# One queue in program order: TensorE's matmuls issued as the program emits them

## The chip, the cores and the metric

The kernel runs on one core of a Trainium2 chip. The metric is the device time of one execution in microseconds (us): the median of three runs, and beside it one profiled execution with its trace. A core has engines that run side by side, each with a queue of its own that it works through from front to back: TensorE (PE in the profile; its weight loads are listed as PEld), VectorE (DVE), ScalarE (ACT), GpSimd (POOL) and SyncE (SP, which here issues the DMAs). An instruction that has to wait for another engine holds up everything behind it in its own queue.

## The reference

Two layers of a hybrid backbone over 256 latent and 256 context tokens of width 1024, all in float32. The core of one layer is this:

```python
def _layer(xl, xc, mod_l, mod_c, P, rope_a, rope_b, ctx_out):
    ...
    hl = _rmsnorm(xl, P['norm_mix']) * (1 + sc1) + sh1
    hc = _rmsnorm(xc, P['norm_mix']) * (1 + csc1) + csh1
    y_l, y_c = _mixer(hl, hc, P, rope_a, rope_b, ctx_out)
    xl = xl + g1 * y_l
    xl = xl + g2 * _conv_ffn(_rmsnorm(xl, P['norm_ffn']) * (1 + sc2) + sh2, P)
    ...
```

`_mixer` makes one input projection, feeds it to three token mixers (A: windowed attention with a sink, 8 heads; B: latent attention, 8 heads; C: gated linear attention in both directions), projects each mixer's output, merges the three by sigmoid gates and projects once more. `_conv_ffn` is an up-projection to 5632 columns, a width-3 convolution over the tokens, silu times value, and a down-projection. In the second (last) layer only the latent tokens are finished, so its later stages run on 256 columns where those of the first run on 512.

## The kernel before

**Work.** Activations lie with features on the 128 partitions and tokens along the columns. Almost all of TensorE's work is `mm3` (lines 171 to 174): a float32 product is made of three products of high and low parts, `whi` by `hh`, `whi` by `hl` and `wlo` by `hh`, so lines 172, 173 and 174 hold three matmuls each time. `load_w` (158) fetches a weight tile by DMA into a ring, ACT casts it to its high part (`whi`, 164) and DVE or POOL subtracts for the low part (`wlo`, 168). `unit` (176) is one output tile: 4 or 8 blocks of 128 rows, three matmuls each, into one bank of PSUM. An activation is split in the same way (`split`, 187).

**Stages of a layer, in the program's order.** The modulation and norm with the first seven output tiles of the input projection (380 to 397); the gated linear attention (434 to 755), with its gates at 537 to 549, where for each of two `t` and two directions `d` a matmul (541) writes half of a PSUM pair that ACT (543) and DVE (544) read; attention A and attention B (796 to 914, called at 983 and 987); the third merge (992); the output projection (1025 to 1039); the up-projection with convolution (`inner`, 1116) and the down-projection (1141 to 1152). A norm is spread over its neighbours as steps: `sums` (228, matmuls of line 233), a chain of small DVE operations (`rsqrt`, 192, and line 239), `spread` (241, the matmul of line 242), then `hmod` for each of 8 tiles.

**What sets the order.** The program emits its instructions in the order of its Python loops. A scheduler then fixes each engine's queue: it goes through the instructions with a machine model, prefers the one emitted first, and lets a later one go ahead on an engine while the earlier one's inputs are not ready by that model. So a queue of the kernel before is the program's order, except where a later instruction overtook. `tc.issue_after(ins)` pins some DMAs and DVE operations of the modulation behind one named instruction; it doesn't name TensorE's.

**Attention's order.** `scores` (803) emits the matmuls of lines 813 and 817 and the softmax behind them on DVE and ACT (819 to 834). `values` (837) emits the transposes of the probabilities (850), which ACT and DVE turn into `pth` (854) and `ptl` (855); `outputs` (858) emits their products (866, 869). `fills` are units of the gates and branch products (`merge`, 771), laid between them by hand:

```python
for i, stp in enumerate(steps + [None]):
    if stp is not None:
        scores(*stp)
        ...
        step_on()
        ...
    pv = values(*steps[i - 1]) if i else None
    for n in range(nfill[i]):
        fills.pop(0)()
        if n == 0 and pv:
            pv()
            pv = None
        ...
```

`pv` is `outputs` of the step before; `step_on` emits the next head's keys, values or queries. So the program's order is: scores of this step, transposes of the step before, one fill, outputs, one more fill.

The change touches the function below and, by the queue that it sets, every matmul that `hybrid` emits.

## Time and profile before

| what | value |
|---|---|
| median of 3 runs | 1519.2 us (1518.48 to 1521.23) |
| profiled execution | 1519.25 us |
| its span, first to last instruction | 1517.5 us |
| TensorE (PE) busy | 1438.5 us, 95% |
| VectorE (DVE) busy | 1218.2 us, 80% |
| ScalarE (ACT) busy | 811.7 us, 53% |
| GpSimd (POOL) busy | 494.6 us, 33% |
| DMA | 213 MB, 139 GB/s over the span |
| mean granted clock of TensorE | 0.981 |

The profiled execution lies 0.05 us from the median, and 1.75 us of it lie outside the span. Busy time counts an engine's own instructions. A timeline lists one engine's instructions in the order of time, so it shows the queue itself; where an engine sat idle before an instruction, the row says for how long and what released it. "PEclk" is the granted share of TensorE's 2.4 GHz: 1.00 or 0.50 in a stretch.

### The profile page before, as it was taken

Reading aid. Unit: us, or ns where it says so; the run is one execution under the profiler, and the core shown is the slowest. Engines: PE = TensorE matmul, PEld = TensorE weight load, DVE = VectorE, ACT = ScalarE, POOL = GpSimd, SP = SyncE. Lnnn points to the kernel's source line nnn. Section 1 sums busy time; section 2 is a strip of 40 time slices with the busy share of each in tenths; the row PEclk is TensorE's granted clock in tenths of the full one; section 3 lists DMA queues with packets and bytes.
Section 4 is the critical chain, followed back from the end, with each engine's and each line's share of the span. In section 5 each row is a group of like instructions: output and inputs, shape, how many; then the busy total and the mean of one; then the engine's idle time right before and its main releaser. Section 6 shows DMA issues by size and latency. Waiting matters only on the chain. (4 is left out here: it accounts for less than half of the span.)

```text
span 1517.5 us, 27758 instructions
## 1 busy us (share of the span) xinstructions
PE 1438.5 (95%) x10062; PEld 1243.2 (82%) x10062; DVE 1218.2 (80%) x2289; ACT 811.7 (53%) x1698; POOL 494.6 (33%) x407
## 2 busy tenths in 40 slices
PE   6988999999999899999999999988989899989997
PEld 4766867778788799788888889967878889989997
DVE  5688597786888979798877979978777886897886
ACT  4565355565653346534244235675466776665663
POOL 0065233233320001446544640034354443133231
PEclk9999999999999999999999999999999999999999
DMA  8411122222236575444645865532132235556553
GB/s 315 169 50 62 46 76 78 72 74 77 84 105 224 178 229 182 139 158 149 214 139 157 289 232 153 182 105 79 56 102 85 89 108 186 179 163 198 175 172 93
DMA packets 107432, 213.28 MB, mean 141 GB/s; under 512 B 12000, under 2 KB 21600, under 8 KB 106272
## 3 DMA queue, kind: packets, MB, share of 16 engines
q1 hardware_dynamic: 106608, 210.86, 42.6%
q8 instruction: 79, 1.29, 0.3%
q10 hardware_dynamic: 688, 0.66, 0.1%
q14 instruction: 57, 0.47, 0.1%
HBM read 210.42 MB, written 1.05 MB: 139 GB/s over the span
## 5 line engine op out<-in xcount | busy, mean ns | idle before, releaser
L168 POOL TENSOR_TENSOR wlo<-raw,whi 128x512 fp32r<-128x512 f32 (+1 forms) x270 | 373.8, 1390 | 711.5 <-ACT whi L164 464.0
L164 ACT CAST whi<-raw 128x512 fp32r<-128x512 f32 (+1 forms) x614 | 360.5, 597 | 320.0 <-PE ps_mm L173 136.4
L172 PE MATMUL ps_mm<-hh,whi 128*128 128x512 f32 (+1 forms) x808 | 298.3, 369 | 11.7 <-ACT cvr L473 8.5
L173 PE MATMUL ps_mm<-hl,whi 128*128 128x512 f32 (+1 forms) x808 | 292.7, 362 | 0.0
L174 PE MATMUL ps_mm<-hh,wlo 128*128 128x512 f32 (+1 forms) x808 | 292.4, 362 | 0.2 <-DVE wlo L168 0.2
L168 DVE TENSOR_TENSOR wlo<-raw,whi 128x512 fp32r<-128x512 f32 (+1 forms) x344 | 238.1, 703 | 44.0 <-ACT whi L164 39.3
L172 PEld LDWEIGHTS ps_mm<-hh,whi 128*128 128x128 f32 x808 | 155.4, 192 | 38.9 <-ACT cvr L473 8.7
L174 PEld LDWEIGHTS ps_mm<-hh,wlo 128*128 128x128 f32 x808 | 154.9, 192 | 26.0 <-DVE wlo L168 0.6
L173 PEld LDWEIGHTS ps_mm<-hl,whi 128*128 128x128 f32 x808 | 155.4, 192 | 23.8 <-issue 0.4
L104 DVE SCALAR_TENSOR_TENSOR jk<-wm,sil 128x1024 f32<-128x1024 f32 x112 | 172.8, 1543 | 1.5 <-DMA wm<-wmod 0.4
L172 PE MATMUL ps_pair<-hh,whi 128*128 128x512 f32 (+1 forms) x312 | 109.8, 353 | 2.0 <-DVE cy L1092 1.7
L174 PE MATMUL ps_pair<-hh,wlo 128*128 128x512 f32 (+1 forms) x312 | 109.0, 352 | 0.3 <-DVE wlo L168 0.2
L173 PE MATMUL ps_pair<-hl,whi 128*128 128x512 f32 (+1 forms) x312 | 109.2, 351 | 0.0
L854 ACT CAST pth<-ps_pair 128x512 fp32r<-128x512 f32 (+1 forms) x96 | 49.4, 515 | 38.7 <-PE ps_pair L850 26.9
L172 PEld LDWEIGHTS ps_pair<-hh,whi 128*128 128x128 f32 x312 | 58.5, 188 | 11.6 <-ACT whi L164 3.2
L174 PEld LDWEIGHTS ps_pair<-hh,wlo 128*128 128x128 f32 x312 | 58.4, 188 | 9.6 <-DVE wlo L168 0.7
L855 DVE TENSOR_TENSOR ptl<-ps_pair,pth 128x512 fp32r<-128x512 f32 (+1 forms) x96 | 57.4, 597 | 10.8 <-ACT pth L854 10.2
L173 PEld LDWEIGHTS ps_pair<-hl,whi 128*128 128x128 f32 x312 | 58.6, 188 | 8.7
L172 PE MATMUL ps_mm<-ach,whi 128*128 128x256 f32 (+1 forms) x200 | 63.7, 319 | 1.2 <-ACT ach L1125 0.7
L173 PE MATMUL ps_mm<-acl,whi 128*128 128x256 f32 (+1 forms) x200 | 63.5, 317 | 0.0
L174 PE MATMUL ps_mm<-ach,wlo 128*128 128x256 f32 (+1 forms) x200 | 63.4, 317 | 0.0
L174 PE MATMUL ps_mm<-mh,wlo 128*128 128x256 f32 x192 | 55.4, 289 | 4.7 <-DVE wlo L168 4.7
(673 smaller groups left out, 3582.2 us busy)
## 6 DMA issues: line engine op xcount, KB each, us to landing
raw<-wup SPq DMA_DIRECT2D x184, 256.0 KB, 3.0
raw<-win SPq DMA_DIRECT2D x182, 256.0 KB, 2.7
wm<-wmod SPq DMA_DIRECT2D x72, 512.0 KB, 3.9
raw<-wdn SPq DMA_DIRECT2D x88, 256.0 KB, 2.9
raw<-wbr SPq DMA_DIRECT2D x48, 256.0 KB, 2.6
raw<-wout SPq DMA_DIRECT2D x48, 256.0 KB, 3.0
wm<-wm SPq DMA_DIRECT2D x8, 1024.0 KB, 8.1
x<-xT SPq DMA_DIRECT2D x16, 256.0 KB, 4.8
```

The costliest lines, as they stand in the source:

```text
L104: V.scalar_tensor_tensor(out=jk, in0=wm, scalar=1.0, in1=sil[:, s], op0=ALU.mult, op1=ALU.mult, accum_out=MOD[l][:, s, t:t + 1])
L164: S.copy(hi[:, :ncols], raw[:, :ncols])
L168: e.tensor_tensor(out=lo[:, :ncols], in0=raw[:, :ncols], in1=hi[:, :ncols].bitcast(F32), op=ALU.subtract)
L172: mm(o, ah, bh, start=start, stop=False)
L173: mm(o, ah, bl, start=False, stop=False)
L174: mm(o, al, bh, start=False, stop=stop)
L854: S.copy(dh, tv)
L855: V.tensor_tensor(out=dl, in0=tv, in1=dh.bitcast(F32), op=ALU.subtract)
```

## The change

TensorE's whole queue is issued in the order in which the program emits its matmuls. The other engines' queues, and the DMAs', are still made by the scheduler, now against that order. No instruction is added or taken away in the source.

```diff
--- before.py
+++ after.py
@@ -1286,7 +1286,7 @@
     arrays = _pack(inputs)
     aps = {k: nc.dram_tensor(k, a.shape, mybir.dt.from_np(a.dtype), kind="ExternalInput").ap() for k, a in arrays.items()}
     out = nc.dram_tensor("out", (KT, 128, T), F32, kind="ExternalOutput").ap()
-    with tile.TileContext(nc) as tc:
+    with tile.TileContext(nc) as tc, tc.manual_schedule(engines={mybir.EngineType.PE}):
         hybrid(nc, tc, aps, out)
     r = run_bass_kernel_spmd(nc, [arrays], core_ids=[0])
     o = r.results[0]["out"]
```

## Rows read from the trace of the kernel before

**Rows 1.** TensorE's waits: line, releaser: us in total, times, longest

```profile
PE ps_o L242 <- DVE dg L239: 8.1, 5, 3.6
PE ps_pair L850 <- DVE ptl L855: 1.7, 2, 1.5
PE ps_pair L172 <- DVE cy L1092: 1.7, 1, 1.7
```

**Rows 2.** Busy us by stretch: length, PE, PEld, DVE, ACT, POOL, PEclk, DMA share, GB/s

```profile
215.00:470.00 255.00, 250.25 (x1315) 203.98 (x1314) 195.04 (x416) 151.70 (x364) 75.93 (x63) 1.00 0.29 93
1085.00:1236.00 151.00, 134.74 (x978) 120.78 (x977) 125.03 (x242) 100.97 (x241) 65.37 (x49) 0.98 0.28 91
```

**Rows 3.** Timeline (start us, us, engine, line, operation) of PE, attention A of layer 0

```profile
222.20 0.50 PE L172 MATMUL ps_mm<-hh,whi 128*128 128x512 f32 x1
...
223.55 1.06 PE L850 MATMUL ps_pair<-cst,p 128*128 128x128 f32 x8 [0.15 <-DVE ptl L855]
```

**Rows 4.** Timeline of PE, the last such place of attention B, layer 0

```profile
447.82 0.28 PE L813 MATMUL ps_pair<-kh,q 96*128 96x256 f32 x1
...
448.31 0.45 PE L869 MATMUL ps_o<-ptl,vb 128*64 128x256 f32 x2
```

**Rows 5.** Timeline of PE, the spread of two norms

```profile
590.13 0.28 PE L172 MATMUL ps_pair<-hh,whi 128*128 128x256 f32 x1
...
592.61 0.67 PE L242 MATMUL ps_o<-dg,ones 128*128 128x256 f32 x2
...
968.90 0.70 PE L242 MATMUL ps_o<-dg,ones 128*128 128x256 f32 x2 [0.24 <-DVE dg L239]
```

**Rows 6.** Timeline of PE, the start of the last down-projection of layer 0

```profile
921.85 0.28 PE L172 MATMUL ps_pair<-ach,whi 128*128 128x256 f32 x1
...
925.94 0.39 PE L172 MATMUL ps_mm<-ach,whi 128*128 128x256 f32 x1 [0.69 <-ACT ach L1125]
```

**Rows 7.** Timeline of PE, the way into attention A of layer 1

```profile
1084.37 0.47 PE L172 MATMUL ps_mm<-hh,whi 128*128 128x256 f32 x1
...
1089.18 0.44 PE L749 MATMUL ps_pair<-cst,osb 128*128 128x128 f32 x2 [1.94 <-DVE osb L717]
...
1095.71 0.86 PE L813 MATMUL ps_pair<-kh,q 128*128 128x512 f32 x2
...
1102.91 0.73 PE L813 MATMUL ps_pair<-kh,q 128*128 128x512 f32 x2 [2.19 <-ACT p L828]
```

**Rows 8.** Timeline of PE and DVE where attention A hands over to B, layer 1

```profile
1166.60 0.39 PE L172 MATMUL ps_mm<-ych,whi 128*128 128x256 f32 x1 [0.37 <-ACT m L778]
...
1170.92 1.04 PE L850 MATMUL ps_pair<-cst,p 128*128 128x128 f32 x8
...
1169.27 0.74 DVE L782 SCALAR_TENSOR_TENSOR m<-m,ps_mm 128x256 f32<-128x256 f32 x2
1170.01 0.69 DVE L855 TENSOR_TENSOR ptl<-ps_pair,pth 128x512 fp32r<-128x512 f32 x1
```

**Rows 9.** Timeline of PE, DVE and ACT, the gates of layer 0

```profile
71.83 0.63 PE L541 MATMUL ps_pair<-cg,wg 96*128 96x512 f32 x2
...
74.40 0.47 PE L541 MATMUL ps_pair<-cg,wg 96*128 96x512 f32 x1
...
73.57 1.41 DVE L544 TENSOR_SCALAR mn<-ps_pair,pp 128x512 f32<-128x512 f32 x2 [0.38 <-ACT lab L543]
...
76.59 2.01 ACT L546 ACTIVATE lab<-lab 128x1024 f32<-128x1024 f32 x2
...
84.35 0.79 PE L172 MATMUL ps_mm<-hh,whi 128*128 128x512 f32 x1 [4.05 <-ACT cvr L473]
```

**Rows 10.** Busy us by stretch at the lower clock: first, last, sum of ten

```profile
83.30:90.10 6.80, 5.75 (x14) 4.49 (x15) 6.80 (x7) 2.87 (x7) 5.85 (x4) 0.50 0.00 0
...
1339.40:1342.80 3.40, 3.40 (x18) 3.40 (x18) 2.72 (x8) 2.11 (x6) 0.00 (x0) 0.50 0.02 6
sum 51.00, PE 45.65 PEld 37.42 DVE 44.46 ACT 21.20 POOL 22.35; mean PE 4.56 PEld 3.74 DVE 4.45 ACT 2.12 POOL 2.24
```

## The prediction

> **What bounds the kernel now.** I read the page's list of engines first: TensorE is busy 1438.5 of 1517.5 us, DVE 1218.2, nothing else above 53%. So TensorE has 79 us of idle time in the whole span, and only what changes its queue's idle time or its clock can change the time by much. Then TensorE's waits: they are many and short, and come from DVE and ACT chains, such as the norm's `dg` or the `ptl` that frees a pair of banks [rows 1]. Then the stretches: the attention of layer 0 has TensorE busy 250.25 of 255 us, that of layer 1 only 134.74 of 151, with DVE at 125.03 [rows 2]. Last the whole timeline of TensorE, laid beside the loops: where does the queue leave the program's order? In 48 stretches that hold 1,111 of its 9,059 matmuls; the other 7,948 stand where the program emits them, and the change moves none of them against its neighbours. In nearly every one of the 48 the pattern is that of [rows 3]: by the program the transposes (850) of the step before come next, and the fill unit (172 to 174) after them; in the queue the fill's first matmuls went ahead at 222.20, and the transposes followed at 223.55, as soon as DVE's `ptl` (855) had freed their pair. The fill covered the wait.
>
> **The change part by part.** Nothing is added or removed. Each overtaking matmul goes back behind the one it overtook. Its price is: the moment at which the overtaken matmul's inputs were ready in the trace, less the moment at which TensorE would reach it. The overtakers then run after it instead of during its wait, so on a busy TensorE the wait is lost. It comes back only if TensorE later waits for something that hasn't moved. The queues of DVE, ACT, POOL and SP hold the same instructions; that their order stays is my assumption, bounded below.
>
> Layer 0's attention, nine places. First [rows 3]: reached at 222.1, ready at about 223.5, so 1.4 lost (1.6 with the rest of that place). Last [rows 4]: the second output's `ptl` products are reached at 447.82, where scores went ahead, and start at 448.31: 0.5. All nine worked like this: 1.6, 3.0, 2.9, 0.9, 0.8, 1.5, 2.5, 0.6, 0.4, together 14.2. TensorE is 98% busy here [rows 2], so little can give it back: the wait of 1.7 for `ptl` outside these places [rows 1] and 0.4 of another. I take 12.1.
>
> Norms, two. `spread` of the first is reached at 590.13, and runs at 592.61 when `dg` is ready [rows 5]: 2.4 lost. Its `sums` wait 1.1 us too, but that wait is inside the 2.4, since `dg` follows from `sums`, which start when they did. The second ends at 968.90 in the same way: 2.7, and 0.8 for low parts of weights that come late around it. After the first norm TensorE waits for `cy` 1.7 us and 0.5 for a low part, and DVE's chain towards them starts no later than before [rows 1]; I give back 2.0. Sum 3.9.
>
> The last down-projection of layer 0. By the program its first tile is finished before the second begins; its last block needs `ach`, the last of `inner`. In the queue the second and third tile ran from 921.85, and the block followed at 925.94 [rows 6]. Now TensorE waits the 4.1 us and then has those 27 matmuls still to do: 3.6 after what it waited anyway.
>
> Layer 1's attention. From 1084.37 gate units ran ahead of the transposes of line 749, ready at 1089.18; scores of the first step are ready at 1095.7, those of the second at 1102.91, after 2.2 us of idle time already [rows 7]. These moments hang on DVE and ACT, not on the fills, so the waits don't add up: counted from the second scores, what is left to run puts TensorE 3.6 us behind at 1106.5, not the 9.1 of the two places each by itself. Nine more places follow; the largest is [rows 8], where a product and scores went ahead of transposes ready at 1170.75 and reached at 1166.1: 4.7, less 0.7 that TensorE waited there already. The nine sum to 9.9. But here TensorE is idle 16.3 of 151 us, with DVE at 83% [rows 2], so most of a delay meets a wait that it shortens: I keep a third, 3.3. Sum 6.9, with 13.5 as the upper end.
>
> The gates. For each `t` two matmuls (541) write the halves of a pair; the second half's wait for DVE's reading of the first (544) [rows 9]. Before, both first halves ran at 71.83 and the second halves at 74.40 and 75.18. In program order the second `t` starts only after the first's second half, so ACT and DVE make two rounds one after the other: exp (546) moves from 76.59 to about 77.8, and with it the copy that TensorE waits 4.05 us for [rows 9]. The two stalls of 2.3 us are swallowed by that wait; its end moves by 1.2. Twice, for two layers: 2.4.
>
> The rest (first stage 0.7, both linear attentions 1.8 and 0.5, up-projection of layer 1 0.5, where a delay of 1.4 meets an idle stretch before 1339): 3.5. Four places cost nothing, since the overtaken matmul was ready when reached.
>
> The clock. In ten stretches the granted clock was 0.50, that is 1.2 GHz, each behind a longer or repeated idle time; TensorE was busy 45.65 us of them [rows 10], so half, 22.8 us, is what the low clock cost. New waits of 4.1 [rows 6] and 4.7 [rows 8] are as long as the 4.05 [rows 9] ahead of the first of these stretches. I add two stretches like the one at 1339 (3.40 busy, 1.7 lost [rows 10]): 3.4; the bounds are 0 and five such, 8.5. The Trainium skill's page "TensorE: Matmul & The Clock Gate" (What's actually happening) says that for modelling, the cost of ramping up the clock is under 1% of a typical span. The trace doesn't agree: 22.8 us are 1.5% here. By the page this term would be left out and the forecast would be 3.4 us lower.
>
> Sum: 12.1 + 3.9 + 3.6 + 6.9 + 2.4 + 3.5 + 3.4 = 35.8. One deduction: with fills later, their evacuations no longer stand ahead of the awaited step in DVE's queue, as `m` (782, 0.74 for two) does just ahead of `ptl` in [rows 8]. I take 0.7 off at each of the six waits above 2.5 us: 4.2. That leaves 31.6, on the profiled execution's 1519.25 (0.05 from the median): 1551.
>
> **The rivals.** *Given back*: DVE's chains set the pace, and TensorE's delays in one place shorten its waits in the next. For it: layer 1's 16.3 idle us, and DVE at 80% overall. Against it: TensorE is 98% busy in layer 0's attention, where the largest term lies. If half of the 14.2 and all of layer 1's but 2 us come back, and no clock is lost: 7 + 2 + 2 (norms) + 1.5 + 2.4 + 2 = 17 at most, near 5 at least; about 1530. *Compounding*: each place costs what it does alone, so all 50.7 us of the 48 places are kept, and five stretches of low clock come on top, 8.5: about 1578. *Faster*: the awaited chains get shorter by more than TensorE waits. Scores and transposes reach ACT and DVE ahead of the fills' casts and evacuations, in layer 1's attention above all. It decides where a ready moment comes earlier by more than the wait costs, 1 us at a typical place; if it removes all new waits and half of layer 1's 16.3 idle us, the time is 1519 less 8, 1511. Against it: the awaited moments of [rows 7] follow from matmuls that no fill overtook. *No change*: the order held back nothing that matters, or what is lost is just regained; 1519.
>
> **How the numbers follow.** Forecast (1537 to 1564): 0.56. Given back (1523 to 1537): 0.19. Compounding (above 1564): 0.12. Faster: 0.07. No change within 0.2% (3 us, about what a measurement of this kernel can tell from none): 0.06. So slower 0.87, same 0.06, faster 0.07. For 8 in 10 I leave out faster, no change and the upper half of compounding, 0.19: 1523 to 1577.
>
> **What would show it.** The matmul count stays, and the rows of line 850 come right behind those of 813 and 817 in each step. TensorE's idle time rises from 79 to about 110 us, with most of the rise at lines 850, 869, 242, 172 behind `ach` 1125, and 541 behind 544; stretches at the low clock rise from ten to twelve. The wait for `cvr` (473) gets shorter, and the exps of line 546 later by about 1.2 us. The forecast is wrong if layer 0's attention (from its first scores to the first matmul of line 992's merge) is no longer than before, if DVE's and ACT's queues come out in another order where TensorE waits, or if layer 1's attention grows by more than 14 us.

## The result, and the profile after

The changed kernel takes 1577.5 us (1576.1 to 1579.3) against 1518.8 us before: a ratio of 1.0385, interval 1.0367 to 1.0403, so 58.6 us slower. The forecast was 1551 with 1523 to 1577: right in sign and on where the waits come from, 26 us too low, and just outside the range.

The page of the changed kernel:

```profile
span 1574.6 us, 27756 instructions
PE 1457.9 (93%) x10062; PEld 1259.4 (80%) x10062; DVE 1208.5 (77%) x2289; ACT 815.9 (52%) x1698; POOL 489.0 (31%) x407
```

The span grew by 57.1 us. TensorE's idle time is 116.7 us (1574.6 less 1457.9) where it was 79.0: 37.7 of the 57.1. The other 19.4 us are *busy* time, with the same 10,062 matmuls. Something made the matmuls themselves slower. Two views tell where, and by what.

First, busy time by stage. Columns as in [rows 2]. The stretches end at the same instruction in both traces: gates to first turn (749), the way from there to the first transposes (850), attention of layer 0, then gates to first turn of layer 1, and way in and attention of layer 1. The kernel before:

```profile
71.80:196.10 124.30, 113.75 (x1464) 91.20 (x1462) 95.86 (x170) 64.61 (x123) 55.20 (x56) 0.93 0.18 58
196.10:216.90 20.80, 18.65 (x81) 14.11 (x82) 18.89 (x26) 10.93 (x22) 9.53 (x8) 0.92 0.21 67
216.90:455.50 238.60, 233.85 (x1238) 190.86 (x1237) 184.71 (x400) 144.08 (x351) 74.03 (x62) 1.00 0.26 82
...
993.00:1089.20 96.20, 85.70 (x926) 70.01 (x925) 72.47 (x167) 52.99 (x119) 38.66 (x57) 0.93 0.21 70
1089.20:1246.50 157.30, 142.98 (x1047) 129.12 (x1048) 129.08 (x246) 107.68 (x256) 68.93 (x50) 0.98 0.29 93
```

The changed kernel, the same stages:

```profile
72.90:202.20 129.30, 114.37 (x1463) 91.67 (x1461) 95.29 (x170) 64.91 (x122) 54.81 (x55) 0.93 0.18 54
202.20:230.20 28.00, 21.05 (x81) 15.62 (x81) 18.12 (x28) 11.76 (x23) 10.10 (x8) 0.82 0.21 65
230.20:487.70 257.50, 243.83 (x1238) 198.69 (x1237) 180.52 (x398) 144.71 (x351) 72.97 (x62) 0.95 0.25 75
...
1033.10:1132.70 99.60, 83.67 (x908) 68.40 (x906) 69.46 (x163) 52.56 (x117) 36.55 (x56) 0.93 0.21 65
1132.70:1302.60 169.90, 147.87 (x1064) 133.16 (x1065) 128.87 (x248) 108.71 (x257) 69.75 (x51) 0.95 0.29 86
```

Length less PE gives the idle time of a stage. It rose by 4.4, 4.8, 8.9, 5.4 and 7.7 us in these five. In the attention of layer 0 the same 1,238 matmuls are busy 10.0 us longer, and the granted clock there is 0.95 instead of 1.00. In layer 1's the busy time rose by 4.9, but 17 matmuls more fall into that stage now, and the stage ahead of it has 18 fewer and is 2.0 us less busy. That leads to the second view, the stretches at 0.50 (1.2 GHz), five of seventeen and their sum, against [rows 10]:

```profile
211.80:218.60 6.80, 5.07 (x12) 3.37 (x13) 5.62 (x10) 1.62 (x4) 0.00 (x0) 0.50 0.11 39
269.80:276.60 6.80, 5.96 (x18) 5.07 (x19) 5.74 (x15) 2.17 (x7) 0.00 (x0) 0.50 0.15 40
423.40:440.40 17.00, 14.26 (x50) 11.88 (x49) 10.65 (x21) 8.64 (x19) 1.28 (x1) 0.50 0.12 30
...
955.90:962.70 6.80, 4.82 (x21) 4.52 (x22) 3.37 (x7) 2.07 (x4) 0.00 (x0) 0.50 0.36 109
...
1218.70:1222.10 3.40, 2.82 (x14) 2.85 (x15) 1.26 (x3) 0.59 (x1) 0.42 (x1) 0.50 0.74 220
...
sum 102.00, PE 84.75 PEld 70.62 DVE 72.95 ACT 45.33 POOL 14.25; mean PE 4.99 PEld 4.15 DVE 4.29 ACT 2.67 POOL 0.84
```

Seventeen instead of ten, 102 us instead of 51. Half of the busy time in them is what the clock cost, since fill matmuls of 512 columns that start every 0.23 us at 1.00 start every 0.43 us there: 42.4 us after (84.75 / 2), 22.8 before [rows 10]. The difference, 19.6, agrees with the 19.4 us of extra busy time. It is an account of busy time: how much of it the kernel would win back at the full clock is a question for the experiments. The mean granted clock was 0.965 to 0.971 in the four executions of the changed kernel, 0.978 to 0.986 in those of the kernel before that are on record.

TensorE's waits, columns as in [rows 1]:

```profile
PE ps_o L233 <- DVE acc L223: 16.7, 4, 10.4
PE ps_pair L850 <- DVE ptl L855: 10.3, 5, 5.3
PE ps_o L242 <- DVE dg L239: 8.5, 5, 2.4
PE ps_pair L541 <- DVE mn L544: 8.1, 4, 2.2
PE ps_pair L813 <- DVE q L729: 8.1, 2, 4.5
PE ps_o L869 <- DVE ptl L855: 6.8, 18, 1.1
PE ps_pair L578 <- DVE ex L601: 6.4, 4, 4.7
PE ps_o L866 <- ACT pth L854: 5.9, 5, 2.1
```

The wait of the transposes for `ptl` went from 1.7 [rows 1] to 10.3 us, that of the products (578) for `ex` from 1.9 to 6.4; the waits of 541, and of the first scores (813) for `q` (729), are new. The 10.4 at 233 is the launch, and the wait for `cvr` of [rows 9] is gone.

### The profile page after: what moved, and what is told of

It reads as the page before. It is cut to its first block, busy times and chain, and to the rows that moved or that the text cites. A ratio compares the mean times of both kernels' runs of the same rounds, so it can differ in the third digit from the quotient of the medians.

```text
span 1574.6 us, 27756 instructions
## 1 busy us (share of the span) xinstructions
PE 1457.9 (93%) x10062; PEld 1259.4 (80%) x10062; DVE 1208.5 (77%) x2289; ACT 815.9 (52%) x1698; POOL 489.0 (31%) x407
## 4 chain that ended last, share of the span: by engine, by line
PE 77%; DVE 15%; ACT 4%; issue 2%; DMA 1%; POOL 1%; SPq 0%; DVEq 0%; ACTq 0%; POOLq 0%
PE ps_mm L172 15%; PE ps_mm L173 15%; PE ps_mm L174 15%; PE ps_pair L172 5%; PE ps_pair L174 5%; PE ps_pair L173 5%; PE ps_pair L813 3%; PE ps_pair L850 2%; PE ps_o L172 2%; PE ps_o L173 2%; PE ps_o L174 2%; DVE ptl L855 1%; DVE wlo L168 1%; PE ps_o L869 1%; PE ps_pair L578 1%
## 5 line engine op out<-in xcount | busy, mean ns | idle before, releaser
L168 POOL TENSOR_TENSOR wlo<-raw,whi 128x512 fp32r<-128x512 f32 (+1 forms) x270 | 369.2, 1372 | 745.4 <-ACT whi L164 687.0
L164 ACT CAST whi<-raw 128x512 fp32r<-128x512 f32 x614 | 361.8, 597 | 347.7 <-PE ps_mm L173 155.2
L855 DVE TENSOR_TENSOR ptl<-ps_pair,pth 128x512 fp32r<-128x512 f32 (+1 forms) x96 | 57.5, 599 | 15.6 <-ACT pth L854 14.9
```

Of the source, the lines that this page charges most:

```text
L164: S.copy(hi[:, :ncols], raw[:, :ncols])
L168: e.tensor_tensor(out=lo[:, :ncols], in0=raw[:, :ncols], in1=hi[:, :ncols].bitcast(F32), op=ALU.subtract)
L855: V.tensor_tensor(out=dl, in0=tv, in1=dh.bitcast(F32), op=ALU.subtract)
```

## The experiments

Two theories. Theory 1: each place where the scheduler had let a fill overtake is paid for by itself, as a wait plus a stretch of low clock behind it. Theory 2: the price comes from the queues of DVE and ACT, which came out in another order. The changed kernels' traces differ by up to 3.5 us ahead of the gates, where none is edited; so delays are compared from one instruction to the next, not from the start. The intervals of the runs with one small edit overlap that of the changed kernel (1.0367 to 1.0403), but for the split fills; so what such an edit wins is read from the trace, place by place, and one trace of each kernel shows it.

**The order fixed in the attention loops only.** On the kernel before:

```diff
+            guard = ExitStack()
+            guard.enter_context(tc.manual_schedule(engines={mybir.EngineType.PE}))
             for i, stp in enumerate(steps + [None]):
...
+            guard.close()
             return hd.get(4)
```

> Program order on TensorE only inside the two attention loops of both layers (from the first scores to the last outputs); everywhere else the scheduler's order. Theory 1 (each place pays its own uncovered wait and the low clock behind it): the price is the delay that the changed kernel gathers there, 7 at the way into attention of layer 0, 19 in its two loops, 11 in layer 1: about 37 us, so 1556. Theory 2 (the other engines' queues, remade against the new order over the whole program, carry the excess): the price isn't local; under 25 or over 50 us.

1550.3 us, ratio 1.0202 (1.0180 to 1.0225): 31 us, 6 less than Theory 1 named, but between the 25 and 50 us outside which Theory 2 put it.

**The order fixed everywhere else.** The same guard, opened at the program's start, closed ahead of these loops and opened again behind them:

```diff
+            order[0].close()
             for i, stp in enumerate(steps + [None]):
...
+            order[0] = ExitStack()
+            order[0].enter_context(tc.manual_schedule(engines={mybir.EngineType.PE}))
             return hd.get(4)
```

> The complement: program order on TensorE everywhere but in the attention loops. Theory 1: about 20 us (first stage 1, gates 2, linear attentions 8, last down-projection of layer 0 5.6, norms and first stage of layer 1 2 to 3, up-projection 1), so 1539, and the two prices add up to that of the whole change, 58. Theory 2: they don't add up; the sum is off by 10 us or more.

1543.2 us, ratio 1.0163 (1.0145 to 1.0180): 24 us, 4 more than named. The two halves add up to 56 of the 58.6 us. Idle time rises by 18.7 us in the one (TensorE busy 1452.6 of 1550.3) and 16.4 in the other (1447.0 of 1542.4), 35.1 where the whole change has 37.7; busy time by 14.1 and 8.5, 22.6 where it has 19.4. So the two halves don't hide each other's cost, and the loss isn't one of the program order as a whole. What the other queues add within a half, the sum can't tell. *Given back* (1523 to 1537) is out by the time itself.

**Eight matmuls of no use in one wait.** One step in the middle of attention B has no fill (`nfill[len(steps) // 2] -= 1`), and there TensorE's timeline in the changed kernel reads:

```profile
422.00 0.49 PE L813 MATMUL ps_pair<-kh,q 96*128 96x512 f32 x1 [1.39 <-ACT q L188]
...
424.48 1.06 PE L850 MATMUL ps_pair<-cst,p 128*128 128x128 f32 x4
427.67 0.58 PE L866 MATMUL ps_o<-pth,vb 128*128 128x256 f32 x1 [2.13 <-ACT pth L854]
428.86 0.69 PE L869 MATMUL ps_o<-ptl,vb 128*64 128x256 f32 x2 [0.61 <-DVE ptl L855]
```

The 17 us at 1.2 GHz shown above begin at 423.40: behind the wait of 1.39 us and one of 0.21 at 422.95, and ahead of those of 2.13 and 0.61 us, which lie inside the stretch. The edit to the changed kernel:

```diff
                 pv = values(*steps[i - 1]) if i else None
+                if not last and not masked and nfill[i] == 0:
+                    warm = psum("mm")
+                    for _ in range(8):
+                        mm(warm, idr, Hh[0], start=True, stop=True)
```

> The changed kernel with 8 extra matmuls of 512 columns (about 1.9 us at 2.4 GHz) into an unused bank, right behind the transposes of the one step of layer 0's attention B that has no fill. There the changed kernel waits 2.1 us for the transposed probabilities and then runs 17 us at 1.2 GHz. Nothing else differs. Theory 1 (the clock is most of the excess): the wait is filled, the stretch at 1.2 GHz gets shorter than 8 us or goes, and TensorE is 4 to 7 us earlier behind it: 1571 to 1574. Rival (a wait costs its own length, the clock costs little): no earlier, or up to 1.9 us later: 1577 to 1579.

1573.7 us, ratio 1.0357 (1.0339 to 1.0375), where Theory 1 had it. Its timeline (908 is the added line), and then its busy time in the stretch that answers to the 17 us above:

```profile
427.75 2.07 PE L908 MATMUL ps_mm<-hh,idr 128*128 128x512 f32 x8
430.54 0.38 PE L866 MATMUL ps_o<-pth,vb 128*128 128x256 f32 x1 [0.71 <-ACT pth L854]
```

```profile
426.50:443.50 17.00, 15.40 (x74) 12.42 (x75) 10.87 (x21) 8.84 (x20) 2.04 (x2) 0.90 0.10 36
```

TensorE does more, and is sooner done: the granted clock is 0.90 instead of 0.50 (the low part is 432.6 to 436.0, as read from the same trace), and against the changed kernel it wins 4.0 us at this place. From the transposes to the first output (866) it takes 3.14 us here and 3.19 us above, so the wait with what fills it is as long. What shrank is the time behind it (3.4 us) and just ahead of it (0.5 us), the clock's share. One thing stays open: the waits of 1.39 and 0.21 us are there as before, and the clock did not fall behind them this time. So the filled wait shows what the low clock costs, and not which wait brought it.

**Half of each fill ahead of the transposes.** The first half of a step's first fill is emitted before `values(i - 1)`, the other behind it:

```diff
                 for n in range(nfill[i]):
-                    fills.pop(0)()
+                    fills.pop(0)(turn if n == 0 else None)
```

(`turn` calls `values` after half of the unit's matmuls.)

> The changed kernel, but the program itself emits the first half of each step's first fill ahead of the transposes and the second half behind them. TensorE still runs in program order. Theory 1: the waits for transposes and for their low parts are covered again; of the 19 us in layer 0's two attention loops at least 10 come back, in layer 1 at least 4: 1556 to 1564. Theory 2: the fill's place doesn't matter much, under 5 us come back: 1572 or more.

1589.7 us, ratio 1.0467 (1.0449 to 1.0484): 12 us slower than the changed kernel instead of 13 to 21 faster, a plain miss for Theory 1. By the number Theory 2 has it (1572 or more), but not by its reason, since the fill's place did matter. Its waits (852, 868 and 871 are the lines 850, 866 and 869):

```profile
PE ps_o L871 <- DVE ptl L857: 10.5, 20, 1.6
PE ps_o L868 <- ACT pth L856: 10.5, 8, 2.2
...
PE ps_pair L852 <- DVE ptl L857: 5.2, 2, 3.9
```

The transposes wait 5.2 us instead of 10.3, the outputs 21.0 instead of 12.7: in all 26.2 against 23.0. As I read it, a fill in program order covers either the chain ahead of the transposes or the one behind them, and half a fill at each covers neither in full; in the kernel before, the scheduler covered both, from whichever unit was ready. These 3.2 us are a part of the price. The span grew by 14.9 us to 1589.5, of which 7.2 are idle time in all and 7.8 busy time; the low clock, now in 21 stretches, makes up some 3 of the latter. The rest isn't explained.

**Matmuls of no use ahead of many waits.** A helper writes n such matmuls into the bank that the waiting instruction will overwrite, or into a free one; 170 of them, at first turns (749), first scores (813), steps with a fill less, `spread` (242), the output projection, the last down-projection and the first product (578). The helper, and one of its places:

```diff
+    def heat(p, n, w=512):
+        w = min(w, p.shape[-1])
+        for _ in range(n):
+            mm(p[:, :w], idr, Hh[0][:, :w], start=True, stop=True)
...
                 yt = one(W)
+                if h == 0:
+                    heat(yt, 6 if NS == 2 else 14)
```

> The changed kernel with matmuls of no use placed on TensorE's queue in front of instructions that wait in its trace (some 26 us of them at the 2.4 GHz level): ahead of the first turn L749 and the first scores L813 of each layer's attention A, ahead of the transposes L850 of each step that has a fill less, ahead of L242 of three norms, of the first matmul of the output projection and of the last down-projection of layer 0, and of the first product L578. The output stays the reference's. Theory 1 (the longer low-clock stretches follow from the waits, and 42.5 us are lost to the low clock against 22.9 in the kernel before): the dummies lie in waits, the low stretches fall from 17 with 102 us to about 10 with 50 to 60 us, and the time goes to about 1564 us (1555 to 1570). Rival (low clock comes and goes without regard to these waits, or the waits are shorter than the dummies): 1577 to 1590 us, with as many low stretches.

1576.0 us, ratio 1.0388 (1.0364 to 1.0411): no gain. The stretches of low clock fell as expected, from 17 and 102 us to 10 and 51 us. But delays against the changed kernel, place by place, split in two: behind the step without a fill of attention B, the output projection, the last down-projection and the way into layer 1 it is earlier by 5.5, 2.3, 2.1 and 1.3 us; at five places where TensorE had not been waiting, or not there (one `spread`, the turn of layer 0, a product, two steps in layer 1), it is later by some 11 us. I had placed those five by the kind of instruction and not by a wait of that instruction in the trace. So the clock's cost fell to about what it was in the kernel before, and the time didn't: TensorE is busy 1471.9 us here, 14 more than without the useless matmuls.

**Only the four that paid.** 72 such matmuls: 8 behind the transposes of the step without a fill, 24 at the output projection, 20 at the last down-projection, 14 and 6 on the way into layer 1.

```diff
-                p = unit(I["wout"][l, j], mh, ml, T, c0=T * s)
+                p = psum("mm", T)
+                if s == 0 and j == 0 and not last:
+                    heat(p, 24)
+                unit(I["wout"][l, j], mh, ml, T, c0=T * s, p=p)
```

> The changed kernel with dummy matmuls only at the places where those of the earlier run lay inside a wait: 8 behind the transposes of the step without a fill in attention B of layer 0, 24 ahead of the output projection and 20 ahead of the last down-projection of layer 0, 14 ahead of the first turn L749 and 6 ahead of the first scores of layer 1. Theory 1 (the low clock behind a wait is what those places cost beyond the wait): the same delays come down that came down in the earlier run, 4 to 5.5, 2.3, 2.1 and 1.3 us, without the cost of the misplaced ones: about 1567 us (1562 to 1571). Rival (those steps were chance, the clock falls elsewhere instead): 1575 to 1580 us.

1571.5 us, ratio 1.0363 (1.0331 to 1.0395): a gain of 6 us by the medians, 3 by the ratios, short of what was expected. So the reading rests on the trace. Three stages of the changed kernel (end of attention B; output projection; feed-forward of layer 0):

```profile
416.50:487.70 71.20, 66.11 (x321) 54.82 (x320) 50.76 (x107) 38.59 (x94) 16.11 (x13) 0.88 0.27 82
487.70:592.90 105.20, 99.38 (x529) 85.86 (x528) 89.73 (x159) 40.81 (x72) 0.00 (x0) 0.97 0.67 213
625.30:977.90 352.60, 348.52 (x1640) 288.88 (x1641) 290.88 (x418) 143.69 (x243) 165.71 (x112) 0.99 0.57 178
```

The same stages with the 72 matmuls:

```profile
417.90:483.70 65.80, 61.86 (x329) 51.01 (x328) 50.63 (x107) 38.48 (x94) 16.12 (x13) 1.00 0.28 92
483.70:586.60 102.90, 99.91 (x555) 86.38 (x553) 88.53 (x159) 40.31 (x72) 0.00 (x0) 1.00 0.66 215
618.90:969.50 350.60, 348.88 (x1660) 289.33 (x1661) 290.82 (x418) 143.78 (x243) 166.72 (x112) 1.00 0.55 179
```

More matmuls in each, and 5.4, 2.3 and 2.0 us less time, at a clock of 1.00. These are the gains of the experiment above again (5.5, 2.3, 2.1), which speaks against chance. So 5.4 and 2.0 us of the loss are shown to be the clock's. The 2.3 at the output projection are the clock's too, but hardly a part of the loss: the kernel before has a wait of 4.70 us for a weight's low part there (5.82 in the changed one), and a low stretch of 6.8 us that begins in it at 530.

**The first fill of attention A emitted ahead of the first scores.** TensorE's timeline in the changed kernel at the way into attention A of layer 0:

```profile
207.59 1.41 PE L749 MATMUL ps_pair<-cst,osb 128*128 128x128 f32 x8
213.53 0.77 PE L813 MATMUL ps_pair<-kh,q 128*128 128x512 f32 x1 [4.53 <-DVE q L729]
```

The edit:

```diff
             fills = list(fills)
+            if masked:
+                fills.pop(0)()
+                nfill[-1] -= 1
```

> The changed kernel with one rearrangement of the program: the first fill of attention A is emitted ahead of the first scores (both layers), and the last step of attention A has a fill less. TensorE's queue is still the program's order. Theory 1 (the place of the fill in the queue set the price of the way into attention): the wait of the first L813 for q, 4.5 us in layer 0 and 3.5 us in layer 1, is covered by 24 matmuls of the fill (5.6 and 2.8 us), and the low stretches at 212 and 1133 us shrink; at the last step about 2.7 and 1 us come back. About 1570 us (1564 to 1576). Rival (the order of the other engines, remade by the scheduler, sets the place): the wait for q stays or moves behind the fill, 1577 us or more.

1573.0 us, ratio 1.0356 (1.0325 to 1.0386). The same place now, with 24 matmuls of the fill between the two rows:

```profile
210.85 1.52 PE L749 MATMUL ps_pair<-cst,osb 128*128 128x128 f32 x8
...
217.82 0.39 PE L813 MATMUL ps_pair<-kh,q 128*128 128x512 f32 x1
```

The wait is gone. By the first transposes 3.8 us are won in layer 0, and 4.1 in the first six steps of layer 1; in layer 1 the last step, which now has a fill less, gives back 3.6. So the fill's place in the queue set this price, as Theory 1 says, and the time is where it was expected. And the chain was no longer than before: from the last multiplication by `rr` (717) to `q` (729) it took 8.1 us in the kernel before, 8.5 after. Theory 2 has next to nothing to explain at this place.

**The step without a fill moved to the end of attention B** (layer 0).

```diff
-            nfill[len(steps) // 2] -= 1
+            nfill[-1 if not masked and not last else len(steps) // 2] -= 1
```

> The changed kernel with one number changed: in attention B of layer 0 the step that has no fill is the last one instead of the one in the middle. Theory 1 (with TensorE in the program's order a step without a fill pays its chains in full, and pays again in the clock behind them): the waits of 1.39, 2.13 and 0.61 us and the 17 us at 1.2 GHz at 420 to 440 us go, some 9 us, and the last step pays about 2.7 us and a shorter stretch of low clock: about 1571 us (1567 to 1575). Rival (the price belongs to a step without a fill wherever it stands): 1576 to 1580 us.

1576.7 us, ratio 1.0383 (1.0359 to 1.0406): the rival's time. In the trace 5.5 us are won behind the old place; at the end outputs wait 0.46 and 0.94 us and a new stretch of low clock begins at 490 us, and 2.9 us are lost again by the first norm. The profiled execution keeps the rest, but it had begun 2.8 us later at the gates, and the medians differ by 0.8 us. Inconclusive.

**The next head's splits emitted behind the transposes.** Where attention A hands over to B in layer 1, PE and DVE of the changed kernel:

```profile
1208.63 1.03 PE L850 MATMUL ps_pair<-cst,p 128*128 128x128 f32 x8
...
1219.28 1.08 PE L850 MATMUL ps_pair<-cst,p 128*128 128x128 f32 x4 [5.28 <-DVE ptl L855]
...
1215.60 0.82 DVE L189 TENSOR_TENSOR q<-qf,q 96x256 fp32r<-96x256 f32 x1
1216.45 0.69 DVE L855 TENSOR_TENSOR ptl<-ps_pair,pth 128x512 fp32r<-128x512 f32 x1
...
1218.46 0.68 DVE L855 TENSOR_TENSOR ptl<-ps_pair,pth 128x512 fp32r<-128x512 f32 x1
```

The pair that the second transposes need is freed by the second `ptl`. Both stand on DVE's queue behind the splits of the next head's keys and queries (189); between them lie an evacuation `m` (782, 0.41 us) and a low part of a weight (168, 1.15 us). The edit:

```diff
-                        if ready:
-                            hd[stp[0] + 1] = ready()
+                        due = ready
                 pv = values(*steps[i - 1]) if i else None
+                if due:
+                    hd[stp[0] + 1] = due()
```

> The changed kernel with one rearrangement: the splits of the next head's queries and keys (the step called ready, L188 and L189 on ScalarE and VectorE) are emitted behind the transposes of the step before and not ahead of them, so that the evacuations L854 and L855 needn't stand behind them. Theory 2 (part of layer 1's attention is paid for the order of VectorE, behind which L850 now waits: 5.28 us at 1214 us, 2.5 us at 268 us): these two waits and the low clock behind them go, some 10 us, and the first scores of a head wait up to 3 us more for their queries: about 1571 us (1566 to 1576). Rival (the waits for queries take the place in full): 1577 to 1583 us.

1573.5 us, ratio 1.0364 (1.0340 to 1.0389). The second transposes now read:

```profile
1214.20 1.06 PE L850 MATMUL ps_pair<-cst,p 128*128 128x128 f32 x8 [2.51 <-DVE ptl L855]
```

5.28 became 2.51, and 2.8 us are won at this place; the wait of 2.5 us at 268 stayed, so of some 10 us expected 4 came. Part of the loss at a handover is DVE's order, then. But that order isn't new: from the one group of transposes to the next it took 10.3 us before (1160.6 to 1170.9, the latter in [rows 8]) and 10.65 after. The chain was as long before; TensorE had other work meanwhile.

**A copy moved, on the kernel before.** TensorE waited 4.05 us for `cvr` there [rows 9], and 4.40 in layer 1.

```diff
-                S.copy(rw, inunit(T_CV + j, NTOK, p))
+                (V.tensor_copy if j == 1 else S.copy)(rw, inunit(T_CV + j, NTOK, p))
```

> The kernel before (scheduler's order on all engines) with one copy moved: the evacuation at line 473 of the second of the four values (j = 1) is done by VectorE instead of ScalarE, where it stood behind the exponentials. Theory 1 (the two waits of 4.06 and 4.40 us for this copy and the low-clock stretches behind them, at 83 and 1005 us, are paid in full): about 1508 us (1504 to 1513). Rival (another reader of the bank, or VectorE's own queue, takes the place of the copy): 1516 to 1522 us.

1518.5 us, ratio 1.0005 (0.9987 to 1.0022). No change, as the rival had it. The unit that had waited for `cvr` starts without a wait at 80.57; the unit behind it now waits nearly as long, for another reader, `scr` of line 466.

```profile
90.77 0.50 PE L172 MATMUL ps_mm<-hh,whi 128*128 128x512 f32 x1 [3.89 <-DVE scr L466]
```

**The copy and matmuls of no use, with the scheduler's order.** The moved copy, and 96 of them in front of waits that precede low clock in the kernel before; then only 34: the 24 of the diff at the output projection above, and these:

```diff
                 yt = one(W)
+                if h == 0 and last:
+                    heat(yt, 10)
```

> The kernel of the moved copy (scheduler's order on all engines) with matmuls of no use in front of the waits that precede its low-clock stretches: first turn L749 of each layer, first scores L813 of layer 1, L242 of three norms, first matmul of the output projection of layer 0, first matmul of the up-projection of layer 1. Theory 1 (a wait of a few us brings the low clock behind it also in the kernel before, some 12 us in all at these places): 3 to 8 us less than with the moved copy alone, about 1503 us. Rival (the low clock is not due to these waits, or the dummies cost more than they give back): the time of the moved copy alone, up to 10 us more.

> The scheduler's order on all engines, the copy at line 473 of the second of the four values on VectorE, and dummy matmuls at two places only: 24 ahead of the output projection of layer 0, 10 ahead of the first turn L749 of layer 1. Theory 1: less than with all the dummies, since those that lay outside waits are left out: 1512 us (1509 to 1516). Rival (the low clock falls elsewhere instead): 1516 to 1519 us, the time of the kernel before.

With 96: 1514.8 us, ratio 0.9981 (0.9970 to 0.9991), low clock down from 51 to 24 us: 3.7 us less than with the copy alone, where 3 to 8 were expected. With 34: 1511.5 us, as expected, ratio 0.9953 (0.9937 to 0.9968), low clock down to 37.5 us. The second beats the kernel before by 0.5%. Which of its edits brings it isn't settled: the delays fall in several stages, some of them without an edit. And the run with less low clock is the slower of the two.

## Why the prediction was wrong

Right: the sign; that on TensorE nothing moves but the overtakers (of 10,062 matmuls by the page, not 9,059); that idle time rises (79 to "about 110", it was 116.7); that the last down-projection waits for `ach` (3.9 us where it had waited 0.7, with 4.1 forecast); that the wait for `cvr` shortens and the exps come later. The second exp (546) starts at 80.36 in the changed kernel's timeline, and the pair ends 1.7 us later than before, counted from the first gate, where 1.2 was forecast.

By terms, idle time of TensorE by stage from the two tables above:

| term | forecast | measured |
|---|---|---|
| attention of layer 0 | 12.1 | 8.9 |
| layer 1: way in and attention | 6.9 | 7.7 |
| gates, linear attentions, way into layer 0's attention | 4.7 | 14.6 |
| norms, last down-projection, the rest | 8.7 | 6.5 |
| deduction | -4.2 | in the rows above |
| clock | 3.4 | 19.4 |
| sum | 31.6 | 57.1 |

**The clock is the step that failed**: 16 of the 25.5 us between the two sums. I took "two stretches like the one at 1339", 3.4 us, because two new waits were as long as the 4.05 us ahead of the first low stretch. Those two are there, at 955.9 and 1218.7, and cost 2.4 and 1.4 us (half of 4.82 and of 2.82), 3.8 together. But eight stretches are new, not two. Two more, at 99.1 and 211.8, follow waits of 4.73 and 4.53 us that the forecast hadn't priced (4.2 us). The other four cost 13.5 us and follow shorter waits: 2.50 us ahead of the one at 269.8; 1.39 and 0.21 ahead of the one at 423.4, which goes on through 2.13 and 0.61; 1.59 ahead of 1000.2; 0.97 and 1.79 ahead of 1242.6. So the step "as long as the 4.05" was wrong as a condition, and the trace of the kernel before could have said so: its low stretch at 165.2 stands behind one idle time of 1.3 us. And the one at 423.4 lost 7.1 us, by itself four times the size that I took for each. The eight come to 21.5 us; the stretches that both kernels have cost 1.9 less than before.

What the experiments confirm of the 19.4 us by filling waits is 5.4 and 2.0 at two places. For the rest the account of busy time stands alone, and in the run with 170 useless matmuls the low clock went down to 51 us and the time stayed, since those matmuls cost about as much as they gave back.

The Trainium skill's page "TensorE: Matmul & The Clock Gate", section "A second HAM failure mode: psum-queue depth-cycling", tells of a kernel in which frequent short idle times between groups of matmuls make the clock go back and forth, which costs throughput. The trace agrees in so far as four low stretches stand behind waits of 2.50 us or less. The forecast had cited only that page's sentence that the ramp is under 1% of a span (What's actually happening), and had called it contradicted by 22.8 us. That sentence is about the first matmuls of a kernel, where both traces show none of it (a granted clock of 1.00 up to the gates), so it says nothing on low stretches inside one; here those come to 2.7% (42.4 of 1574.6).

**The gates, the linear attentions and the way in** were under-sized by 10 us. At the way into layer 0's attention I counted part of the fill that had run in the waits; all 24 matmuls had, 5.6 us at 0.234 each, and the 4.53 us wait shows it. At the gates the step "swallowed by that wait" was right as far as it went: 541 now waits 3.9 us where `cvr` cost 4.05. What came behind it was missed:

```profile
98.83 1.56 PE L578 MATMUL ps_pair<-ex 64*128 64x128 f32 x13 [4.73 <-DVE ex L601]
...
1098.44 0.61 PE L233 MATMUL ps_o<-ones,acc 128*128 128x1 f32 x4 [3.86 <-DVE acc L223]
```

The first products start 4.1 us later than before, counted from the first gate, and the later exps account for 1.8 of that. The other 2.3 are DVE's queue, which came out in another order there. The kernel before, then the changed one:

```profile
92.84 0.68 DVE L601 TENSOR_TENSOR ex<-ex,qk 128x512 f32<-128x512 f32 x1
93.44 1.49 DVE L593 TENSOR_TENSOR ex<-bb 128x256 f32<-128x256 f32 x1
```

```profile
95.53 1.49 DVE L593 TENSOR_TENSOR ex<-bb 128x256 f32<-128x256 f32 x1
96.94 1.75 DVE L601 TENSOR_TENSOR ex<-ex,qk 128x512 f32<-128x512 f32 x1
```

The factor that the products wait for (601) ran ahead of the third subtraction (593), and runs behind it now, 1.07 us more slowly. So "that their order stays" was wrong here, and Theory 2 holds for a part of this place; how much of the whole loss such swaps make up, no run isolates. In layer 1 a norm's `sums` wait 3.86 us where the same place waited 0.20 before. I had followed the chain to one waiter and stopped.

**The deduction** has nothing behind it in the runs. At its own example, the handover, `m` still runs just ahead of the awaited `ptl`, with a weight's low part beside it. And where measured the awaited chains took no less than before: 8.1 and 8.5 us, 10.3 and 10.65 us.

**Layer 1's attention** came out close, 7.7 for 6.9, partly by luck: the handover of [rows 8] cost 5.28 where I kept a third of 4.0, other places less than I kept.

*Compounding* named 1578, and the time is that; but its split is not the one measured. It kept all 50.7 us of the places and 8.5 for the clock. Idle time rose by 37.7, and the clock cost 19.4.

## What to carry to other kernels

Price a new wait on TensorE as wait plus clock: look at short waits too, not only at long ones, and cost the place by the matmuls behind it at 1.2 GHz. In these runs a unit of fill in program order covered the one chain beside which it is emitted, and the step without a fill lost most to the clock (7.1 us). Compare the other engines' queues as well before taking their order as fixed. Idle time and busy time of each stage, beside one another, tell the two costs apart, as long as the stage holds the same matmuls in both traces.

## What the runs showed of the hardware

Matmuls that compute nothing, laid into waits that the trace shows, made three stages 2.0 to 5.4 us shorter, with the granted clock at 1.00 there instead of 0.88 to 0.99. Where TensorE hadn't been waiting they cost time, some 11 us in the run with 170 of them.

In the changed kernel a low stretch (269.8 to 276.6 us) begins in a single wait of 2.50 us, with one of 0.27 us ahead of it:

```profile
270.64 1.73 PE L850 MATMUL ps_pair<-cst,p 128*128 128x128 f32 x7 [2.50 <-DVE ptl L855]
```

And low clock can stand in other places from one trace to the next: with the copy moved, there are stretches at 402 and 1194 us, in places that had none before and where nothing was edited. Whether the edit brought them, or the kernel before has them in some executions, one trace of each doesn't show.
